# Queries, keys and the output projection by Strassen's scheme, in a two-layer encoder on one core

## The chip, the core and the metric

The kernel runs on one core of a Trainium2 chip. Five engines work side by side, each through its own list of instructions: TensorE (PE, matmuls; its weight loads are shown as PEld), VectorE (DVE), ScalarE (ACT), GpSimd (POOL) and SyncE (SP), which here only issues DMAs. They meet through semaphores. The metric is the device time of one execution in microseconds (us).

## What is computed

An encoder of two layers runs on 512 prompt tokens and 256 sample tokens, with 1024 channels. The weights are the same for both, so the kernel holds all 768 tokens together; only the mixers keep them apart. From the reference:

```python
h = rmsnorm(x, norm_mix_g)
proj = jnp.einsum('bsd,dc->bsc', h, w_in)          # 1024 -> 9760 columns
qa, ka, va, qb, kb, vb, rb, glf, glb, ga, gb = jnp.split(proj, IN_SPLIT_POINTS, axis=-1)
ya = mixer_a(qa, ka, va) @ w_branch_a              # attention, 3 groups x 8 heads x 64
yb = mixer_b(qb, kb, vb, rb, glf, glb, ...) @ w_branch_b   # gated linear attention, 4 heads
merged = sigmoid(ga) * ya + sigmoid(gb) * yb
x = x + merged @ w_out
h = rmsnorm(x, norm_ffn_g)
x = x + square(relu(h @ w_ff1)) @ w_ff2            # 1024 -> 4096 -> 1024
```

Mixer A (attention) has three groups of eight heads: a band of 64 neighbours on either side, and bands on the tokens of every 4th and every 16th position. Each group has its own softmax with a distance penalty, and the groups' outputs are weighted by their softmax denominators. Its queries and keys are 1536 columns each. Mixer B (GLA) has four heads of 128 key and 256 value channels, with a decay per channel, run forward and backward in chunks; its queries and keys are 512 columns each. At the end stands a last rmsnorm.

## The kernel before

Each dense product is taken in fp32r, with both operands split into a hi and a lo half, in three passes (hi x hi, hi x lo, lo x hi) for every 128 rows of the contraction. `Norm` keeps the layer's input times the norm's gain as eight pairs of tiles `hh`, `hl` (128 channels x 768 tokens); the factor per token, `nm.r` (along the free axis) or `nm.rt` (per partition), is multiplied in where a product leaves PSUM.

Two forms take a product from that. `feat_dense` (L243) makes tiles of 128 output columns x tokens: the weight is the stationary operand and 512, then 256 tokens (`SPLITS`) or twice 384 (`HALVES`) stream past it, 24 matmuls each. `tok_dense` (L362) makes tiles of 128 tokens x 256 columns, with the tokens stationary. A weight piece comes by one DMA (`raw`, 2 buffers), is cast on ACT (`whi`, L162) and its rest taken on DVE (`wlo`, L108). The second FFN matrix already goes through `quad_dense` (L326) with operands from `Quads` (L274) and `wquad` (L303): the Strassen-Winograd scheme, which takes seven products of half the size in place of eight, at the cost of sums of quarters of both operands.

The order of the work is set by streams. `add` appends a dense product with the makers of its weights to a stream, `make_units` calls the makers some entries ahead, and `dense_piece` issues the next few matmuls. `weave(steps, total)` (L210) walks through the steps of a mixer and after each issues pieces until the share of `total` us is reached, so PE has matmuls between the steps:

```python
while done < total * (i + 1) / len(steps):
    t = dense_piece()
```

A layer goes like this. Six slices of the attention's values (`tok_dense`, to `v_dram`); the GLA decays (to `la_dram`); queries and keys of head pair 0 (`attention_dense`, L484: six column tiles, evacuated with a multiply by r at L497 to L520). Then four times: the steps of head pair p (`attention_steps`, L525) woven with 44 us of queries and keys of pair p + 1 (`weave(steps, 44)`), behind the last with the dense work of GLA head 0. The steps of a pair are: scores (L590 to L596) with a minimum and a biased copy on DVE (L606) and an exponential with a sum on ACT (L609) for each half; `exchange` stores the sums of groups 1 and 2 to `s_dram`; `combine` (L657) loads them in natural order (`sn`), forms the common weights and sends them back through `l_dram`; probabilities (L615), transposes of them on PE (L621), their split (L624), products with the values (L633). Then four GLA heads (`gla_steps`, L741), each woven with the queries, keys, values and gates of the next head (`gla_dense`, L701), the last one with gate A's eight tiles. Then gate B, `w_branch_a`, `w_branch_b`, the output projection (`feat_dense` with `HALVES`, evacuated at L1168), and the FFN in chunks: up (`feat_dense`), down (`quad_dense`).

After the program is recorded in this order, a scheduler sets the order on each engine. Tiles come from pools: `b3` (36 buffers of 128 x 768), small ones for the mixers (`s1`, `k2`, `lr`, and `dist`, the distance table), and `f3`, `ws` for the FFN, which are opened when the mixers' are closed.

Of the kernel before, what the change touches and what calls it, by code (L numbers as in the profile page):

```python
# [16 lines left out]
DM = 1024  # L17
# [19 lines left out]
V_SLICES = tuple((i * 256, 256 + 32 * (i == 5)) for i in range(6))  # L37
# [39 lines left out]
def encoder(ctx: ExitStack, tc: tile.TileContext, a, y_prompt, y_sample):  # L77
# [19 lines left out]

    def k2(name, dt, tag="k2"):
        return scope[tag].tile([128, 2, 256], dt, tag=tag, name=name)
# [28 lines left out]
    def mixer_constants(pool):  # L128
# [10 lines left out]
        scope.update(dist=dist, cumT=cumT, mask=mask,  # L139
                     glT=pool.tile([98, T], F32R, name="glT"),  # L140
                     wgate=pool.tile([98, 1024], F32R, name="wgate"))
# [3 lines left out]
    l_dram = drm.tile([4, T, 2], F32, name="l_dram")  # L145
    x_dram = drm.tile([DM, T], F32, name="x_dram")
# [28 lines left out]
    def add(makers, body):  # L175
        entry = {"makers": list(makers), "units": [], "body": body}
        stream.append(entry)
        pending.extend((entry, m) for m in entry["makers"])

    def make_units(entry, ahead):  # L180
        while pending and (len(entry["units"]) < len(entry["makers"]) or ahead > 0):
            if len(entry["units"]) == len(entry["makers"]):
                ahead -= 1
# [7 lines left out]
    def dense_piece():  # L191
        while True:
            if not current:
# [3 lines left out]
                make_units(entry, 1)  # L197
# [28 lines left out]

    def feat_tile(unit, ci, x, t0, n, i, evac):
# [3 lines left out]
        ts = slice(t0, t0 + n)  # L231
        yield from mm_group(acc, n, len(x), lambda k: [(w[:, k, c], y[:, ts]) for w, y in passes(hi, lo, *x[k])],
                            3 * n / 2400)
# [9 lines left out]
    def feat_dense(w, c0, x, evac, ncol=128, splits=SPLITS):  # L243

        nkt = len(x)
# [28 lines left out]
    class Quads:  # L274
# [3 lines left out]
        def __init__(self, n):  # L278
            self.n = n
            self.x, self.ops = [None] * n, {}  # L280
            self.b11 = None

        def first(self, p, x):
            if self.b11 is None:
                self.b11 = b3("b11h", F32R, (128, 2, HT)), b3("b11l", F32R, (128, 2, HT))
            self.x[p] = x
            self.ops["B11", p] = split2(x[:, 0:HT], *(y[:, p] for y in self.b11))

        def second(self, p, y):
# [3 lines left out]
            t1, t3, t2, t4 = t13[:, 0:HT], t13[:, HT:T], t24[:, 0:HT], t24[:, HT:T]  # L293
            nc.vector.tensor_tensor(t1, b12, b11, op=ALU.subtract)
            nc.vector.tensor_tensor(t3, b22, b12, op=ALU.subtract)
            nc.vector.tensor_tensor(t2, b22, t1, op=ALU.subtract)
            nc.vector.tensor_tensor(t4, b21, t2, op=ALU.subtract)
            for z, names in ((y, ("B21", "B22")), (t13, ("T1", "T3")), (t24, ("T2", "T4"))):
                hi, lo = split2(z, b3("qh", F32R), b3("ql", F32R))
                for i, name in enumerate(names):  # L300
# [951 lines left out]
```

## Time and profile before

| | us |
|---|---|
| median of 3 runs (lowest, highest) | 3004.87 (3003.84, 3006.55) |
| the profiled execution, whole | 3005.5 |
| its span, first to last instruction | 3003.4 |
| PE busy | 2950.8 (98%) |
| PE weight loads busy | 2791.2 (93%) |
| DVE busy | 1943.3 (65%) |
| ACT busy | 1314.0 (44%) |
| POOL busy | 38.3 (1%) |

The profile was taken in one execution. "Busy" is the time in which an engine's instructions run; PE's records overlap, since matmuls are pipelined, so the step from one matmul to the next is read from long runs of them and not from the mean length of a record. A line such as L223 is the line of the kernel that recorded the instruction; helpers such as L108 (a subtraction that leaves the lo half) serve many places, so the tile names tell where one belongs. The names left of the arrow are written, those on its right are read.

### The profile page before, as it was taken

The page shows a single profiled execution, that of the slowest core. Times are in us where ns is not written, and L with a number is a line of the kernel's source. Part 1 is how long each engine was busy: PE and PEld are TensorE (multiplying, and loading weights), DVE is VectorE, ACT ScalarE, POOL GpSimd, SP SyncE. Part 2 cuts the span into 40 slices and gives each one's busy share as a digit, 9 for nine tenths or more (in the row PEclk, how much of TensorE's full clock was granted, in tenths as well). Part 3 has the DMA queues.
Part 4 walks back from the last instruction along what each step waited for, and adds up shares of the span by engine and source line. Part 5 has one row for each costly group of instructions (what it writes and reads, how often), then busy time and mean ns, then how long its engine had stood idle before and what let it go on. Part 6 is the DMA issues. An engine that isn't in the chain of part 4 may idle for free.

```text
span 3003.4 us, 48678 instructions
## 1 busy us (share of the span) xinstructions
PE 2950.8 (98%) x18908; PEld 2791.2 (93%) x18908; DVE 1943.3 (65%) x4177; ACT 1314.0 (44%) x2790; POOL 38.3 (1%) x119
## 2 busy tenths in 40 slices
PE   8999999999999999999999999999999999999998
PEld 7988889999889999999899888999988899999997
DVE  5456667765445777676953666677754557777767
ACT  4556665444223433333453655655542233333334
POOL 1000000000000000000000000000000000000000
PEclk9999999999999999999999999999999999999998
DMA  6533322222332222222254333322233322222222
GB/s 209 195 83 85 92 79 89 64 72 66 132 101 84 63 71 64 64 66 69 90 191 135 81 86 92 90 92 71 58 110 101 105 64 63 64 64 71 71 61 66
DMA packets 391318, 268.27 MB, mean 89 GB/s; under 512 B 40464, under 2 KB 364464, under 8 KB 391088
## 3 DMA queue, kind: packets, MB, share of 16 engines
q1 hardware_dynamic: 391088, 265.16, 29.8%
q8 instruction: 149, 2.44, 0.3%
q14 instruction: 81, 0.66, 0.1%
HBM read 217.77 MB, written 47.33 MB: 88 GB/s over the span
## 4 chain that ended last, share of the span: by engine, by line
PE 91%; DVE 3%; DMA 3%; ACT 2%; issue 1%; SPq 0%; POOL 0%; DVEq 0%; ACTq 0%
PE acc L223 68%; PE wA L341 8%; PE wC L341 4%; PE wB L341 2%; PE op L633 2%; PE go L850 1%; PE pt L621 1%; PE up L828 1%; PE cp L772 1%; PE ap L810 1%; DMA sn<-s_dram 1%; ACT whi L162 1%; PE sp L596 1%; DVE xT L1206 1%; DMA l_dram<-b 1%
## 5 line engine op out<-in xcount | busy, mean ns | idle before, releaser
L223 PE MATMUL acc<-hh,whi 128*128 128x384 f32 (+2 forms) x2560 | 873.7, 341 | 0.0
L223 PE MATMUL acc<-hl,whi 128*128 128x384 f32 (+2 forms) x2560 | 860.0, 336 | 0.0
L223 PE MATMUL acc<-hh,wlo 128*128 128x384 f32 (+2 forms) x2560 | 859.5, 336 | 0.0
L223 PEld LDWEIGHTS acc<-hh,wlo 128*128 128x128 f32 x2560 | 482.8, 189 | 32.0
L223 PEld LDWEIGHTS acc<-hh,whi 128*128 128x128 f32 x2560 | 483.6, 189 | 26.6
L223 PEld LDWEIGHTS acc<-hl,whi 128*128 128x128 f32 x2560 | 483.9, 189 | 23.0
L162 ACT CAST whi<-raw 128x1024 fp32r<-128x1024 f32 x256 | 268.9, 1050 | 372.8 <-PE acc L223 222.5
L223 PE MATMUL acc<-whi,hh 128*128 128x256 f32 (+1 forms) x1344 | 389.1, 290 | 2.4 <-DVE vst L1004 1.4
L223 PE MATMUL acc<-whi,hl 128*128 128x256 f32 (+1 forms) x1344 | 383.1, 285 | 3.0 <-DVE hl L395 2.8
L223 PE MATMUL acc<-wlo,hh 128*128 128x256 f32 (+1 forms) x1344 | 383.1, 286 | 0.8 <-POOL wlo L108 0.8
L108 DVE TENSOR_TENSOR wlo<-raw,whi 128x1024 fp32r<-128x1024 f32 (+1 forms) x253 | 309.8, 1225 | 84.6 <-ACT whi L162 81.8
L223 PEld LDWEIGHTS acc<-whi,hl 128*128 128x128 f32 x1344 | 258.6, 192 | 5.0 <-DVE hl L395 3.6
L223 PEld LDWEIGHTS acc<-whi,hh 128*128 128x128 f32 x1344 | 258.1, 192 | 4.0 <-issue 2.4
L223 PEld LDWEIGHTS acc<-wlo,hh 128*128 128x128 f32 x1344 | 257.9, 192 | 1.5 <-POOL wlo L108 1.1
L1191 DVE SCALAR_TENSOR_TENSOR rl<-acc,nr 128x384 f32<-128x384 f32 x128 | 70.9, 554 | 187.4 <-PE acc L223 186.1
L1192 ACT ACTIVATE hq<-rl 128x384 f32<-128x384 f32 x128 | 67.1, 524 | 198.3 <-DVE rl L1191 198.2
L1206 DVE TENSOR_TENSOR xT<-xT,wA 128x384 f32<-128x384 f32 x256 | 136.0, 548 | 20.8 <-PE wA L341 19.3
L270 ACT CAST sh<-s 128x512 fp32r<-128x512 f32 x128 | 78.1, 619 | 142.3 <-DVE s L315 80.2
L108 DVE TENSOR_TENSOR ptx<-pt,ptx 128x256 fp32r<-128x256 f32 x192 | 81.0, 422 | 81.8 <-ACT ptx L624 79.3
L223 PE MATMUL acc<-spl,whi 128*128 128x256 f32 (+1 forms) x384 | 129.4, 337 | 0.0
L223 PE MATMUL acc<-sph,whi 128*128 128x256 f32 (+1 forms) x384 | 129.3, 337 | 0.0
L223 PE MATMUL acc<-sph,wlo 128*128 128x256 f32 (+1 forms) x384 | 129.0, 336 | 0.0
(272 smaller groups left out, 5480.6 us busy)
## 6 DMA issues: line engine op xcount, KB each, us to landing
raw<-in_w_in SPq DMA_DIRECT2D x152, 512.0 KB, 3.8
raw<-in_w_ff SPq DMA_DIRECT2D x64, 512.0 KB, 4.1
v_dram<-vst SPq DMA_DIRECT2D x72, 256.0 KB, 3.4
raw<-in_w_ff SPq DMA_DIRECT2D x64, 256.0 KB, 2.9
raw<-in_w_ff SPq DMA_DIRECT2D x128, 128.0 KB, 2.9
v<-v_dram SPq DMA_DIRECT2D x64, 128.0 KB, 4.6
raw<-in_w_branch_b SPq DMA_DIRECT2D x16, 512.0 KB, 4.0
raw<-in_w_out SPq DMA_DIRECT2D x16, 512.0 KB, 4.2
```

Of the source, the lines that this page charges most:

```text
L108: eng.tensor_tensor(out, x, hi.bitcast(F32), op=ALU.subtract)
L162: nc.scalar.copy(hi, raw)
L223: nc.tensor.matmul(acc[:, :n], wt, xt, start=(k == 0 and j == 0), stop=(k == nkt - 1 and j == 2))
L270: nc.scalar.copy(hi, x)
L341: nc.tensor.matmul(acc[:, :HT], x, y, start=(new and p == 0 and j == 0), stop=(p == quads.n - 1 and j == 2), skip_group_check=True)
L596: nc.tensor.matmul(sp[hh][:, (g - 1) * 128:g * 128], q[g][pb, bs], k[g][pb, bs], start=True, stop=True)
L621: nc.tensor.transpose(pt[:, g, hh, :], pr[hh][:, g * 128:(g + 1) * 128], ident)
L633: nc.tensor.matmul(op[:, hh], v[:, hh].rearrange("p s c -> p (s c)"), pT[g][:, hh].rearrange("p s c -> p (s c)"), start=(g == 0), stop=(g ...
L772: nc.tensor.matmul(cp[:, j, :], x[:, j, dc], scope["cumT"][:, d, :], start=(i == 0), stop=(i == 1))
L1191: nc.vector.scalar_tensor_tensor(r, acc[:, :n], 0.0, fnorm.r[:, t0:t0 + n], op0=ALU.max, op1=ALU.mult)
L1192: nc.scalar.activation(q[0][:, t0:t0 + n], r, AF.Square)
L1206: nc.vector.tensor_tensor(x, x, acc, op=ALU.add)
```

## The change

Queries and keys of both mixers (32 column tiles in a layer) become a stage of their own between the first value slices and the attention. `Quads(4)` forms the Strassen operands of the normalised input (x times gain times r, so no product needs r later), and `long_dense` takes two column tiles at a time, a unit: seven products of 4 x 3 matmuls of 384 columns, in the three banks A, B and C, with the weight's sums on DVE and a split for each product. `projections` adds the parts up and stores each finished tile to `p_dram`.

```diff
+    def long_dense(w, units_of, quads, use):
...
+        def load(m):
+            if m % 2:
+                z = [scope["ws"].tile([128, 4, 128], F32, tag="ws", name="wr") for _ in range(4)]
+            else:
+                y = [wraw.tile([128, 8, 128], F32, tag="raw", name="raw8") for _ in range(2)]
...
+        def maker(m, an):
...
+                if m < last and an == "A12":
+                    load(m + 1)
...
+                if an == "S1":
+                    r["S3"] = scope["ws"].tile([128, 4, 128], F32, tag="ws", name="s3")
+                    nc.vector.tensor_tensor(r["S3"], r["A11"], r["A21"], op=ALU.subtract)
+                    nc.vector.tensor_tensor(r["A21"], r["A21"], r["A22"], op=ALU.add)
...
+                op = wsp.tile([128, 8, 128], F32R, tag="w", name="aop")
+                return split2(r[an], op[:, 0:4], op[:, 4:8])
...
+        def product(m, name, bn, bank):
...
+                for p in range(n):
+                    bh, bl = quads.ops[bn, p]
+                    for j, (x, y) in enumerate(passes(ah[:, p], al[:, p], bh, bl)):
+                        nc.tensor.matmul(acc[:, :HT], x, y, start=(new and p == 0 and j == 0),
+                                         stop=(p == n - 1 and j == 2), skip_group_check=True)
...
+                use(m, name, acc[:, :HT])
...
+        for m in range(last + 1):
+            own = [(m, p) for p in ((p1, p2, p5, p6, p3) if m == 0 else (p1, p5, p2, p6, p3))]
+            if m:
+                own.insert(1, (m - 1, p7))
+                own.insert(4, (m - 1, p4))
...
+    def projections(units):
...
+        def total(m, i, half, acc, t):
...
+                elif scale is None:
+                    nc.vector.tensor_tensor(dst, at(acc), at(t), op=ALU.add)
+                else:
+                    nc.vector.scalar_tensor_tensor(dst, at(acc), scale, at(t), op0=ALU.mult, op1=ALU.add)
+            if i != half:
+                nc.sync.dma_start(out=p_dram[row * 128:(row + 1) * 128, :], in_=held.pop((m, i)))
...
+        def normalised(k, x):
+            nc.vector.scalar_tensor_tensor(x, x, gmix[:, l, k:k + 1], nm.r, op0=ALU.mult, op1=ALU.mult)
...
+        long_dense(w_in, [(u[0][0], u[1][0]) for u in units], ops, projections([[c[1:] for c in u] for u in units]))
+        weave(steps, 40 if l else 30)
+        while len(stream) > 7 * len(units):
             dense_piece()
```

The mixers read the finished tiles back. `attention_load` replaces `attention_dense`; its loads and the hi/lo split of group 0 are five steps that are put among the later steps of the pair before, and the load of `sn` is moved ahead of the last three score steps of the band. What fills PE beside the mixers is other dense work: three of the six value slices and gate A's first four tiles (stored to `p_dram`, since the buffers are needed) come beside the head pairs, GLA values and gates beside the GLA heads. These read the same operands through `h_at`, which no longer need a multiply by r. The mixers' pools open only after the new stage, as the stage uses `f3` and `ws`.

```diff
-        return (by_two([u[0] for u in units[1]]) + [exchange] + [u[0] for u in units[0]] + [combine] + [lambda: None] * 4 +
-                skewed([u[1] for kind in (0, 1) for u in units[kind]], 1) + [finish])
+        later_steps = skewed([u[1] for kind in (0, 1) for u in units[kind]], 1)
+        for i, step in enumerate(following):
+            later_steps.insert(8 + 9 * i, step)
+        return (by_two([u[0] for u in units[1]]) + [exchange] + [u[0] for u in units[0][:3]] + [natural] +
+                [u[0] for u in units[0][3:]] + [combine] +
+                [lambda: None] * 4 + later_steps + [finish])
...
+            if p == 0:
+                values(1, False, h_at, False)
+                values(3, False, h_at, False)
+            elif p == 1:
+                values(5, False, h_at, False)
+                gate_a(0, True)
+            elif p == 2:
+                for j in range(1, 4):
+                    gate_a(j, True)
             else:
-                gd = gla_dense(0, w_in, nm, gn)
-            weave(steps, 44)
+                gd = gla_dense(0, w_in, h_at, gn)
+            weave(steps, 24 if p in (1, 2) else 32)
```

The output projection takes the same scheme: `branch_b` in the order 0, 4, 1, 5, 2, 6, 3, 7 forms `merged = Quads(4)`, and `long_dense` has four units, whose products are added to x as they come. The gates' tiles are taken in halves of 384.

```diff
-        feat_dense(a["w_out"][l], 0, mg, evac, ncol=DM, splits=HALVES)
+        long_dense(a["w_out"][l], [(m * 128, (m + 4) * 128) for m in range(4)], merged, use)
```

Two places show what that does to PE's own list of instructions. The first is the scores of the second head pair (first layer): `sp` are scores, `acc` a dense tile. Before:

```order
L596 MATMUL sp<-qk 128x128 x8
L223 MATMUL acc<-hh,whi 128x512
L223 MATMUL acc<-hl,whi 128x512
L223 MATMUL acc<-hh,wlo 128x512
L223 MATMUL acc<-hh,whi 128x512
L223 MATMUL acc<-hl,whi 128x512
L223 MATMUL acc<-hh,wlo 128x512
L596 MATMUL sp<-qk 128x128 x8
```

Now (L737 and L731, L733 are the scores of the dilated groups and of the band; the dense work is a value slice):

```order
L232 MATMUL acc<-whi,ql 128x256
L232 MATMUL acc<-wlo,qh 128x256
L232 MATMUL acc<-whi,qh 128x256
L232 MATMUL acc<-whi,ql 128x256
L737 MATMUL sp<-qk 128x128 x16
L731 MATMUL sp<-qk 128x192
L733 MATMUL sp<-qk 128x192
L731 MATMUL sp<-qk 128x192
L733 MATMUL sp<-qk 128x192
L232 MATMUL acc<-wlo,qh 128x256
L731 MATMUL sp<-qk 128x256 x2
L733 MATMUL sp<-qk 128x256 x2
```

Eight scores stood between runs of six dense matmuls of 512 columns; now 20 follow one another, with single dense matmuls of 256 columns between the next ones.

The second place is the second GLA head of the first layer: `up` are the state updates of the scan, `go` its outputs. Before:

```order
L223 MATMUL acc<-whi,hh 128x256
L223 MATMUL acc<-whi,hl 128x256
L223 MATMUL acc<-wlo,hh 128x256
L828 MATMUL up<-vh,kdh 128x256
L828 MATMUL up<-vl,kdh 128x256
L828 MATMUL up<-vh,kdl 128x256
L223 MATMUL acc<-whi,hh 128x256
```

Now:

```order
L965 MATMUL up<-vh,kdl 128x256
L965 MATMUL up<-vh,kdh 128x256
L965 MATMUL up<-vl,kdh 128x256
L965 MATMUL up<-vh,kdl 128x256
L232 MATMUL acc<-whi,b11l 128x256
L232 MATMUL acc<-wlo,b11h 128x256
L232 MATMUL acc<-whi,b11h 128x256
L232 MATMUL acc<-whi,b11l 128x256
L987 MATMUL go<-vh,ah 128x256
L987 MATMUL go<-vl,ah 128x256
L987 MATMUL go<-vh,al 128x256
L987 MATMUL go<-sh,qh 128x256
```

Updates came in threes, one state's, with dense work on both sides; now several states' stand in a row, and four dense matmuls lie between them and the outputs.

## Rows read from the trace of the kernel before

**Rows 1.** The busy time of each engine (its share of the span, its instructions), and the clock that TensorE was granted in 40 equal slices of the span (tenths, 9 is 0.9 or more).

```profile
PE 2950.8 (98%) x18908; PEld 2791.2 (93%) x18908; DVE 1943.3 (65%) x4177; ACT 1314.0 (44%) x2790; POOL 38.3 (1%) x119
...
PEclk9999999999999999999999999999999999999998
```

**Rows 2.** The chain of waits in order of time: start in us, length in us, engine, tile and line of a piece, and how many instructions it has.

```profile
89.61 13.30 PE acc L223 x111
...
734.35 258.54 PE acc L223 x1494
...
1069.52 24.96 PE acc L223 x144
```

**Rows 3.** TensorE's instructions by line, operands and shape, over the whole run: count, busy time, mean ns of one, idle time just before them. In a shape, 128x512 is a matmul that streams 512 columns. `hh`, `hl` are the hi and lo halves of the normalised input, `mgh`, `mgl` those of the merged branches, `whi`, `wlo` those of a weight. One row of three is shown for each shape; the other two passes have the same counts.

```profile
L223 PE MATMUL acc<-hh,whi 128*128 128x512 f32 x768 | 309.5, 403 | 0.0
...
L223 PE MATMUL acc<-hh,whi 128*128 128x256 f32 x768 | 220.9, 288 | 0.0
...
L223 PE MATMUL acc<-mgh,whi 128*128 128x384 f32 x256 | 85.5, 334 | 0.0
```

**Rows 4.** Busy time of each engine in stretches of the run (start:end, length, then each engine's busy us with its instructions, granted clock, share and rate of the DMA engines). The stretches are the second head pair of the first layer, its second GLA head, a chunk of its FFN, 20 us at the end of its FFN, and 20 us in the second layer's attention.

```profile
257.20:329.60 72.40, 69.65 (x457) 60.67 (x456) 49.47 (x141) 43.86 (x129) 3.85 (x14) 1.00 0.34 88
534.90:601.90 67.00, 67.00 (x521) 64.97 (x520) 47.10 (x121) 33.59 (x85) 0.00 (x0) 1.00 0.24 72
...
1069.50:1132.50 63.00, 63.00 (x362) 62.25 (x361) 46.51 (x84) 21.76 (x33) 0.00 (x0) 1.00 0.23 68
...
1480.00:1500.00 20.00, 17.74 (x87) 16.19 (x88) 19.42 (x41) 11.56 (x22) 0.00 (x0) 0.91 0.31 112
1740.00:1760.00 20.00, 17.68 (x116) 15.08 (x116) 9.86 (x48) 13.82 (x52) 2.38 (x8) 1.00 0.56 137
```

**Rows 5.** What TensorE waited for, over the whole run: its tile and line, the engine and line that ended the wait, us in total, number of waits, the longest.

```profile
PE sp L596 <- DVE s L606: 7.4, 8, 1.0
PE pt L621 <- ACT t L615: 6.2, 6, 2.3
...
PE wA L341 <- DVE xT L1206: 5.4, 5, 1.6
...
PE op L633 <- DVE ptx L108: 1.6, 4, 0.8
```

**Rows 6.** The timeline of the second head pair of the first layer: start, length, engine, line, operation (a wait before it in brackets). First TensorE with the pair's first scores (L596) and first transposes of probabilities (L621), then ScalarE with two neighbouring exponentials of the statistics (L609) from the start of the row of 24.

```profile
257.17 1.16 PE L596 MATMUL sp<-qk 64*128 64x128 f32 x16
...
279.29 0.76 PE L621 MATMUL pt<-eye,t 128*128 128x128 f32 x4 [0.70 <-ACT t L615]
...
260.57 0.51 ACT L609 ACTIVATE junk<-t,s 128x256 f32<-128x256 f32 x1
...
262.01 0.49 ACT L609 ACTIVATE junk<-t,s 128x256 f32<-128x256 f32 x1
```

**Rows 7.** The chain of waits inside 255 to 300 us, from the statistics of the second head pair to its probabilities.

```profile
269.84 1.85 DMA s_dram<-s
...
271.82 3.75 DMA sn<-s_dram
...
276.28 1.04 ACT whi L162
277.35 1.23 DVE wlo L108
```

**Rows 8.** VectorE's instructions in the second head pair (257.2 to 329.6 us) by line and shape: the weight splits, and the first and the last of the eight rows in which queries and keys leave PSUM (L518, L520, L497, L500).

```profile
L108 DVE TENSOR_TENSOR wlo<-raw,whi 128x1024 fp32r<-128x1024 f32 x6 | 7.3, 1224 | 1.2 <-ACT whi L162 1.2
...
L518 DVE SCALAR_TENSOR_TENSOR qk<-acc,qsc,nr 128x512 f32<-128x512 f32 x2 | 2.3, 1140 | 0.0
...
L500 DVE TENSOR_TENSOR qkx<-acc,nr 128x256 f32<-128x256 f32 x1 | 0.4, 425 | 0.0
```

**Rows 9.** The same view of the second GLA head (534.9 to 601.9 us): weight splits, the two lines that end in a multiply by r and a gate (L722, L732), and the first and the last of the four rows in which queries and keys leave PSUM.

```profile
L108 DVE TENSOR_TENSOR wlo<-raw,whi 128x1024 fp32r<-128x1024 f32 x6 | 7.3, 1224 | 2.7 <-ACT whi L162 2.7
...
L732 DVE SCALAR_TENSOR_TENSOR gt<-th,rt,gn 128x256 f32<-128x256 f32 x6 | 2.9, 484 | 0.2
L722 DVE SCALAR_TENSOR_TENSOR vl<-acc,rt,vh 128x256 fp32r<-128x256 f32 x6 | 2.9, 481 | 1.2 <-ACT vh L721 1.2
...
L713 DVE TENSOR_TENSOR gqk<-acc,nr 128x512 f32<-128x512 f32 x1 | 0.7, 684 | 0.0
...
L713 DVE TENSOR_TENSOR gqk<-acc,nr 128x256 f32<-128x256 f32 x1 | 0.4, 415 | 0.0
```

**Rows 10.** Durations over the whole run of the kinds of operation that the new stage is made of, on VectorE (a split of a 128x512 weight sum, of 128x768 and of 128x384, a sum of 128x384) and on ScalarE (a cast of 128x512, a 128x384 pass out of an accumulated tile).

```profile
L108 DVE TENSOR_TENSOR sl<-s,sh 128x512 fp32r<-128x512 f32 x128 | 87.8, 686 | 9.2 <-ACT sh L270 5.5 <-PE wA L341 2.9
...
L108 DVE TENSOR_TENSOR ql<-hq,qh 128x768 fp32r<-128x768 f32 x32 | 30.4, 950 | 0.0
...
L108 DVE TENSOR_TENSOR b11l<-hq,b11h 128x384 fp32r<-128x384 f32 x32 | 17.8, 555 | 5.0 <-ACT b11h L270 4.9
...
L294 DVE TENSOR_TENSOR t<-hq 128x384 f32<-128x384 f32 x32 | 17.5, 548 | 0.0
...
L270 ACT CAST sh<-s 128x512 fp32r<-128x512 f32 x128 | 78.1, 619 | 142.3 <-DVE s L315 80.2 <-PE wA L341 30.7 <-DVE s L318 16.0
...
L1192 ACT ACTIVATE hq<-rl 128x384 f32<-128x384 f32 x128 | 67.1, 524 | 198.3 <-DVE rl L1191 198.2
```

More of the change, by code (lines that the diff above doesn't have):

```diff
@@ L230, in feat_tile @@
         c = slice(ci * 128, (ci + 1) * 128)
-        ts = slice(t0, t0 + n)
-        yield from mm_group(acc, n, len(x), lambda k: [(w[:, k, c], y[:, ts]) for w, y in passes(hi, lo, *x[k])],
-                            3 * n / 2400)
+        yield from mm_group(acc, n, NK if callable(x) else len(x),
+                            lambda k: [(w[:, k, c], y) for w, y in passes(hi, lo, *cols(x, k, t0, n))], 3 * n / 2400)
         evac(i, t0, n, acc)
@@ L525, in attention_steps, with load, others, begin @@
-    def attention_steps(p, q, k):
-        c = p * 128
+        raw = {}
+        def load(tile_, which, g):
+            row = which * 12 + g * 4 + p
+            nc.sync.dma_start(out=tile_, in_=p_dram[row * 128:(row + 1) * 128, :])
+        def others(which):
+            for g in (1, 2):
+                (q, k)[which][g] = b3("qk")
+                load((q, k)[which][g], which, g)
+        def begin(which):
+            raw[which] = b3("qkx")
+            load(raw[which], which, 0)
+        def stacked(which):
+            lst = (q, k)[which]
+            lst[0] = [b3("qk", F32R) for _ in range(2 + 2 * which)]
+            x = raw[which]
+            for hh in range(2):
+                pb, other = slice(hh * 64, hh * 64 + 64), slice(64 - hh * 64, 128 - hh * 64)
+                hi = lst[0][hh]
+                nc.scalar.copy(hi[pb], x[pb])
+                if which:
+                    nc.gpsimd.memset(lst[0][2 + hh][other].bitcast(F32), 0.0)
+                    nc.scalar.copy(hi[other], x[pb])
+                sub((lst[0][2 + hh][pb] if which else hi[other]), x[pb], hi[pb])
@@ L960, in load_x @@
             for j in range(n // 128):
-                t = rows[j, half] = start.tile([128, 512], F32, tag="xin", name="xin")
+                t = rows[j, half] = b3("xin", shape=(128, 512))
                 nc.sync.dma_start(out=t, in_=src[j * 128:(j + 1) * 128, half * 512:(half + 1) * 512])
@@ L1015, in evac @@
                 nc.vector.tensor_copy(gx[:, 96:98], ones[:, 0:2])
[L1016 to L1018 removed]
+            tok_dense(parts, nco, x, evac, order)
+        for i, low_rank in ((0, False), (4, True), (2, False)) if l == 0 else ((4, True), (2, False), (0, False)):
+            values(i, low_rank, nm.h, True, (4, 5, 0, 1, 2, 3) if l == 0 else tuple(range(NT)))
         prefetch()
```

476 lines of the change are left out of this document (293 added, 183 removed).

## The prediction, made before the result was known

> **What bounds the kernel now.** I read the share of busy time first: TensorE (PE) 2950.8 of 3003.4 us, 98%, at nearly the full granted clock, while VectorE (DVE) has 65% and ScalarE (ACT) 44% [rows 1]. So the time is the number of matmul columns that PE streams, plus some 50 us in which PE waits. The chain of waits in order of time gives the price of a column from long runs in which nothing else ends: 111 matmuls of 256 columns in 13.30 us (119.8 ns each), 1494 of alternating 512 and 256 in 258.54 us (173.05 ns), 144 of 384 in 24.96 us (173.33 ns) [rows 2]. The three agree: 0.45 to 0.47 ns a column, so a matmul of 384 costs what a mean one of the 512/256 pair costs, and only the count of matmuls matters. The table of forms gives the counts [rows 3]. The busy time by stage shows where PE has no slack and where the others are near it [rows 4]; the list of PE's waits shows what it waited for [rows 5]. Most of the 15.2 us in attention come from the scores' statistics, the transposes and the value products (7.4 + 6.2 + 1.6).
>
> **What goes: matmuls.** The forms with 512 and 256 columns count 768 each for each of three passes [rows 3], 4608 matmuls. They belong to 48 column tiles in each layer (32 of queries and keys, 16 of the gates), 48 to a tile, so queries and keys of both layers have 2/3 of them: 3072. Times 173.05 ns: 531.6 us. The new stage takes them two column tiles at a time: 16 units per layer, each 7 products of 12 matmuls of 384 columns, 2 x 16 x 84 = 2688, times 173.33 ns = 465.9 us. Gain 65.7. The output projection has 3 x 256 matmuls of 384 [rows 3] and becomes 2 layers x 4 units x 84 = 672: 96 fewer, 16.6 us. The gates change from 512 + 256 to 384 + 384 columns: nothing. Together -82.3. The profiled execution took 3005.5 us (span 3003.4 and 2.1 around it), 0.6 above the median of 3004.87; the sum is made against 3005.5: 2923.2 if every wait stays as it is.
>
> **What it costs: cover.** Queries and keys were also the dense work that filled PE while a head pair's softmax went through DVE, ACT and memory. They are now done ahead, and each stretch has less to fill it.
>
> Attention. A pair now takes 72.4 us with 69.65 of PE [rows 4]; its 288 dense matmuls x 173.05 ns are 49.8, so PE's own work for a pair is 19.8 and 2.8 are waits. The new code gives the four pairs two value slices (288 x 119.8 ns = 34.5), a value slice and a gate tile (17.3 + 8.3), three gate tiles (25.0), and the first GLA head's values and gates (34.5). The chain that counts runs from a pair's first scores to its first transposes of probabilities: 257.17 to 279.29, 22.1 us [rows 6], of which the statistics of 24 halves on ACT at 0.49 us are the larger part, then a store and reload of the sums (1.85 and 3.75 us) and the combine, in which a weight's split stood (1.04 + 1.23 us) [rows 7]. The program before put 45 matmuls of 512 and 24 of 256 on PE in that stretch: 45 x 226.3 ns (2 x 173.05 - 119.8) + 24 x 119.8 = 13.1 us, and the scores themselves about 7.3 (22.1 less the 13.1 and 1.7 of waits). By the order of the new program that stretch holds 12 matmuls of 384 and 90 of 256 in the first pair (12.9 us), 53 of 256 in the second (6.4), 32 of 384 in the third (5.5), 77 of 256 in the fourth (9.2), and in the last three also three value products of the pair before (0.4). The chain itself gets shorter, as the reload is queued before the last scores and fewer weight splits stand in it: between 18 (3.4 us start, 24 x 0.49, and some 3 for bubbles and the combine) and 22.1 as now; I take 20. PE's program reaches the transposes after 20.2, 14.1, 13.2 and 16.9 us, so it waits 0, 5.9, 6.8 and 3.1, and with the 1.1 of smaller waits that a pair has now, 20.2 per layer, 40.4 in all against 15.2: **+25** (at 18: +10; at 22.1: +42). In the second pair DVE has 49.5 - 9.4 (the eight evacuation rows of queries and keys) - 3 x 1.224 (splits) + 3 (value splits, gate copies) = 39.4 of 45.4 us, 87% [rows 8]: full, not over.
>
> GLA heads. A head takes 67.0 us with no wait [rows 4]; without its 96 query and key matmuls (16.6) 50.4. DVE's 47.1 lose two weight splits (2.4), the evacuations of queries and keys (2.2) and the multiply by r (about 0.7): 41.8 [rows 9], 83%. The nearest rows are an FFN chunk with DVE at 74% where PE lost nothing and the 20 us from 1480 with DVE at 97% where PE lost 2.26 us, 11% [rows 4]. Between them by the share, 83% loses 4.4%, 2.2 us a head; the order shows the updates of several states in a row with no dense work between them, which speaks for a loss. I take 2: **+16** for 8 heads (bounds 0 and 5.7 a head, the 11%).
>
> Clock. In the 20 us from 1480 the granted clock was 0.91, in those from 1740, with as little PE work, 1.00 [rows 4]: not the share decides but how the idle time lies. One such drop costs 1.8 us (0.09 x 20). The four longest new waits (second and third pair, both layers) may each bring one; I take half: **+4** (0 to 7). The Trainium skill ("TensorE: Matmul & The Clock Gate", section "HAM oscillation — how this bites in real kernels") says that a kernel which makes PE wait in every round pays for the cold clock in every round. By that rule all 16 pairs and heads would pay: 29 us in place of 4, a rival below; the 1.00 from 1740 speaks against it for short waits, and the longer ones have no row here.
>
> Handover. Before the new stage the normalised input is formed and split: per pair of rows 2 x 950 ns, one split of 555, four sums of 550 and three splits of 950 ns, 7.5 us, 30 us of DVE in all [rows 10], woven into 30 us (layer 1) or 40 us (layer 2) of value work that itself has some 9 to 12 us on DVE. Layer 1 is up to 9 us late, of which the first two products cover 4; layer 2 about in time. **+6** (0 to 16). After the last product, the distance table is fetched into memory that the stage held: **+4** for two layers (0 to 10, a transfer of 3.75 us [rows 7] and its issue). The merged operands before the output projection: the last pair's 7.5 us of DVE lie behind the last branch tile, partly under the first products, **+4** (0 to 10).
>
> The new stage itself: a unit is 84 x 173.33 = 14.56 us of PE against seven splits (686 ns), four sums of the same size and some 2.3 of totals on DVE, 9.9 us, 68%; ACT seven casts (619) and four copies (524), 6.4 [rows 10]. That is below the FFN chunk's 74%, where nothing was lost: 0 (upper bound 11%, 1.6 a unit). Its weights, 1 MB per unit in 14.6 us, are 72 GB/s, and the 32 stores of 384 KB a layer lie under it. The loads of queries and keys for a pair are issued during the pair before, 20 us and more ahead of use, and cost nothing.
>
> Sum: 2923.2 + 25 + 16 + 4 + 6 + 4 + 4 = **2982 us**, 0.8% faster: of 82 us of matmuls taken away some 59 come back as waits.
>
> **The rivals.**
> A, everything stays hidden: the recorded order puts other work into the waits, only the matmuls go. For it: GLA and FFN rows without any wait [rows 4]. Against it: the 22.1 us chain with 14 us on top of it. 2923 with all waits as before, up to 2950 with the attention term alone.
> B, slower: the mixers' chains become the bound. If the attention chain keeps its 22.1 (+42) and each GLA head loses 11% of its time (5.7, +46), with the other terms as taken the time is 2923 + 42 + 46 + 4 + 14 = 3029. With attention as forecast it is slower than before from 4.9 us a head: (82.3 - 25 - 4 - 14) / 8. For it: DVE at 83 to 87% with ACT in turn with it; against it: no wait at all now in the heads.
> C, the stage of queries and keys is bound by DVE, ACT or weights: 1 us a unit is 32 us, 3014. For it: the products of the FFN waited 5.4 us for one kind of sum [rows 5]; against it: that is under 0.1 us for each of their 64 groups.
> D, the cold clock after every wait: 2982 + 25 = 3007.
> That the change does not do what it says can be left out: the order holds the 2688 and 672 matmuls.
>
> **How the numbers follow.** Forecast 0.52 (its own range 2950 to 2999; 0.50 faster, 0.02 the same), A 0.21 (faster), B 0.14 (0.02 same, 0.12 slower), C 0.08 (0.02, 0.03, 0.03), D 0.05 (0.01, 0.02, 0.02). About 0.2% is what a measurement of this kernel can tell from no change: 2999 to 3011. So faster 0.74, same 0.09, slower 0.17. The range, 2922 to 3025, reaches to A's lower end and to B's near end.
>
> **What would show it.** Right: PE busy near 2870, PE idle near 110 us in all; from first scores to first transposes 18 to 20 us in the second and third pair with a PE wait of 5 to 7 just before; heads of 51 to 54 us; units of the new stage at 14.6 us. Wrong: heads over 56 us or a clock under 0.95 over a whole head (B, D); units over 15.5 us (C); transposes without a wait (A).

## The result and the profile after

The changed kernel takes 3025.47 us (median of 4 runs, 3024.01 to 3028.84) against 3005.71 for the kernel before in the same series: a ratio of 1.0068, 95% interval 1.005 to 1.0085. It is slower, where 0.8% faster was forecast. The page of the profiled execution (span, busy times, granted clock in 40 slices) answers to [rows 1]:

```profile
span 3024.6 us, 49070 instructions
...
PE 2912.0 (96%) x18428; PEld 2832.2 (94%) x18428; DVE 2151.7 (71%) x4607; ACT 1447.1 (48%) x3104; POOL 38.4 (1%) x119
...
PEclk9999999999999999999999999999999999999998
```

PE is busy 39 us less on the page, where 82.3 us of matmuls went, and the span is 21 us longer. PE's idle time grew from 52.6 to 112.6 us (span less busy), and the mean granted clock of the span fell from 0.995 to 0.986. To see where the time lies I cut both runs at the same places of the program: the first matmul of the second layer, and in each layer the first attention score, the first GLA matmul, the first matmul of branch A, the first product of the second FFN matrix. The columns are those of [rows 4]. Before, first and second layer:

```profile
0.00:186.80 186.80, 174.40 (x1224) 163.73 (x1224) 86.10 (x173) 81.07 (x150) 10.45 (x15) 0.98 0.56 179
186.80:474.40 287.60, 280.73 (x1933) 250.49 (x1933) 197.92 (x572) 180.77 (x522) 12.45 (x48) 1.00 0.33 85
474.40:788.50 314.10, 314.10 (x2254) 296.49 (x2253) 204.59 (x500) 147.89 (x354) 0.00 (x0) 1.00 0.27 84
788.50:1031.50 243.00, 243.00 (x1398) 227.03 (x1397) 127.08 (x195) 77.73 (x117) 0.00 (x0) 1.00 0.26 80
1503.80:1664.70 160.90, 160.90 (x1180) 153.97 (x1180) 76.00 (x147) 66.70 (x117) 2.94 (x8) 1.00 0.50 162
1664.70:1953.30 288.60, 280.11 (x1933) 250.46 (x1933) 198.14 (x572) 180.96 (x522) 12.45 (x48) 1.00 0.33 85
1953.30:2267.40 314.10, 314.10 (x2253) 296.44 (x2253) 204.09 (x499) 147.96 (x354) 0.00 (x0) 1.00 0.27 84
2267.40:2510.40 243.00, 243.00 (x1398) 227.05 (x1397) 127.11 (x195) 77.73 (x117) 0.00 (x0) 1.00 0.27 80
```

After:

```profile
0.00:332.10 332.10, 309.38 (x1834) 302.62 (x1834) 235.33 (x414) 169.94 (x314) 9.04 (x9) 0.98 0.49 157
332.10:564.80 232.70, 211.31 (x1612) 201.25 (x1612) 157.66 (x525) 165.53 (x506) 13.93 (x54) 0.96 0.52 155
564.80:811.10 246.30, 236.23 (x1771) 232.89 (x1770) 171.39 (x466) 130.80 (x342) 0.00 (x0) 0.97 0.33 107
811.10:1047.20 236.10, 235.97 (x1350) 221.72 (x1349) 154.69 (x250) 88.70 (x136) 0.00 (x0) 1.00 0.26 78
1521.00:1823.60 302.60, 294.74 (x1794) 291.23 (x1794) 223.87 (x388) 154.20 (x281) 1.47 (x2) 0.99 0.46 148
1823.60:2050.50 226.90, 210.38 (x1612) 200.78 (x1612) 157.91 (x525) 165.37 (x506) 13.93 (x54) 0.97 0.53 159
2050.50:2296.80 246.30, 235.67 (x1772) 232.35 (x1771) 171.33 (x465) 131.05 (x342) 0.00 (x0) 0.98 0.33 107
2296.80:2532.80 236.00, 236.00 (x1350) 221.81 (x1349) 154.88 (x250) 88.81 (x136) 0.00 (x0) 1.00 0.26 78
```

Read the length of each stretch against the matmuls that moved, at the prices of [rows 2], for one layer. "Lost" is by how much the stretch is longer than that, for both layers together.

| stretch | matmuls moved | measured, layer 1 and 2 | lost |
|---|---|---|---|
| values, queries and keys | +233.0 (new stage) - 49.8 (pair 0) - 51.8 (three slices) = +131.4 | +145.3, +141.7 | 24.2 |
| attention | - 149.5 - 16.6 + 51.8 + 33.3 = -81.0 | -54.9, -61.7 | 45.4 |
| GLA heads to gate B | - 49.8 - 33.3 = -83.1 | -67.8, -67.8 | 30.6 |
| branches, output projection, first FFN tiles | -8.3 | -6.9, -7.0 | 2.7 |
| rest | 0 | +1.5, -1.2 | 0.3 |

The stretches lose 103 us together; 82.3 of matmuls went. That is the 21 us. The list of PE's waits (whole run) says where the idle part of it lies; it answers to [rows 5]:

```profile
PE acc L232 <- ACT sgb L618: 20.4, 2, 10.5
PE pt L762 <- ACT t L756: 19.5, 6, 4.6
PE pt L762 <- issue: 8.1, 2, 4.5
PE op L774 <- DVE ptx L117: 6.3, 12, 1.8
PE acc L232 <- DVE gx L1155: 6.2, 4, 3.9
...
PE wA L431 <- ACT u L475: 3.9, 2, 2.0
```

The first line is new. The second and third were 6.2 us in all, the fourth 1.6.

Five stretches of the changed kernel settle some of the forecast's conditions: the stage of queries and keys, the GLA heads, and three places just behind a wait.

```profile
110.00:332.00 222.00, 221.10 (x1265) 220.10 (x1264) 154.06 (x242) 115.97 (x208) 1.47 (x2) 1.00 0.46 150
566.00:757.50 191.50, 191.34 (x1523) 188.41 (x1522) 152.01 (x434) 110.36 (x307) 0.00 (x0) 1.00 0.29 88
360.00:363.40 3.40, 3.40 (x18) 3.40 (x17) 1.27 (x3) 3.05 (x10) 0.00 (x0) 0.50 0.02 0
470.50:476.00 5.50, 4.97 (x19) 4.83 (x20) 1.74 (x4) 4.36 (x13) 0.00 (x0) 0.50 0.08 2
787.40:793.60 6.20, 6.16 (x19) 6.16 (x20) 0.59 (x1) 0.75 (x2) 0.00 (x0) 0.51 0.01 3
```

The new stage is as forecast: 221.1 of 222.0 us PE is busy. The heads have no wait. Behind these three waits PE works at a granted clock of 0.50, the lower of its two levels, so such a wait costs more than its own length.

### The profile page after: what moved, and what is told of

The parts are those of the page before. It is cut to its first block, busy times and chain, and to the rows that moved or that the text cites. A ratio compares the mean times of both kernels' runs of the same rounds, so it can differ in the third digit from the quotient of the medians.

```text
span 3024.6 us, 49070 instructions
## 1 busy us (share of the span) xinstructions
PE 2912.0 (96%) x18428; PEld 2832.2 (94%) x18428; DVE 2151.7 (71%) x4607; ACT 1447.1 (48%) x3104; POOL 38.4 (1%) x119
## 4 chain that ended last, share of the span: by engine, by line
PE 84%; DVE 6%; DMA 3%; ACT 3%; issue 2%; SPq 1%; POOL 0%; DVEq 0%; ACTq 0%
PE acc L232 44%; PE wA L431 11%; PE wA L357 8%; PE wC L431 5%; PE wC L357 4%; PE wB L431 3%; PE wB L357 2%; PE go L987 1%; PE op L774 1%; PE pt L762 1%; PE sp L737 1%; DMA sn<-s_dram 1%; PE cp L909 1%; DMA raw<-in_w_in 1%; PE ap L947 1%
## 5 line engine op out<-in xcount | busy, mean ns | idle before, releaser
L232 PE MATMUL acc<-hh,whi 128*128 128x384 f32 x1024 | 345.7, 338 | 0.0
L232 PE MATMUL acc<-hh,wlo 128*128 128x384 f32 x1024 | 344.2, 336 | 0.0
L232 PE MATMUL acc<-hl,whi 128*128 128x384 f32 x1024 | 343.7, 336 | 0.0
L170 ACT CAST whi<-raw 128x1024 fp32r<-128x1024 f32 (+1 forms) x176 | 185.4, 1053 | 293.3 <-PE acc L232 184.9
L431 PE MATMUL wA<-qh,aop 128*128 128x384 f32 x960 | 262.6, 340 | 4.9 <-ACT u L475 3.9
L232 PEld LDWEIGHTS acc<-hl,whi 128*128 128x128 f32 x1024 | 192.1, 188 | 0.9 <-DVE hl L546 0.4
L232 PEld LDWEIGHTS acc<-hh,whi 128*128 128x128 f32 x1024 | 192.2, 188 | 0.3
L232 PEld LDWEIGHTS acc<-hh,wlo 128*128 128x128 f32 x1024 | 192.2, 188 | 0.3
L431 PEld LDWEIGHTS wA<-qh,aop 128*128 128x128 f32 x960 | 177.1, 190 | 7.0 <-ACT u L475 4.4
L431 PE MATMUL wC<-qh,aop 128*128 128x384 f32 x640 | 178.3, 337 | 1.2 <-ACT aop L281 1.1
```

The lines of the kernel that those rows point to most:

```text
L170: nc.scalar.copy(hi, raw)
L232: nc.tensor.matmul(acc[:, :n], wt, xt, start=(k == 0 and j == 0), stop=(k == nkt - 1 and j == 2))
L431: nc.tensor.matmul(acc[:, :HT], x, y, start=(new and p == 0 and j == 0), stop=(p == n - 1 and j == 2), skip_group_check=True)
```

## The experiments

All times stand beside runs of the kernel before on the same chip. Since the chips differ a little, kernels are compared by their ratios to it; 0.001 is 3.0 us, and a ratio's interval is 0.001 to 0.002 on either side. The changed kernel has 1.0068.

**What makes gate B wait.** The chain of waits at the end of the first layer's GLA heads, in the changed kernel (start, length, what):

```profile
769.27 0.51 SPq L1343
...
769.83 0.43 SPq L623
...
770.31 6.57 DMA spl<-ma_dram
...
777.00 0.97 DVE spl L626
...
777.99 0.84 ACT sph L628
...
785.18 0.96 DVE spl L626
...
786.90 0.49 ACT sgb L618
```

SP issues three of the four reloads of gate A (L1343) only behind the last stores of the GLA, then the loads of branch A's input (L623). The first of those land at 776.9. VectorE and ScalarE then add and split four tiles, and only behind the fourth does ScalarE come to the first gate tile of gate B (`sgb`), whose bank PE waits for. PE stood from 777.5 to 787.4.

e1_gates:

```diff
-            gate(ta[j], ta[j])
-        xa = [split_from((ma_dram[0], ma_dram[1]), j, f3, f3) for j in range(4)]
+        gate_steps = [f for j in range(4) for f in (lambda j=j: split_a(j), lambda j=j: gate(ta[j], ta[j]))]
...
+        for _ in range(6):
+            dense_piece()
+        weave(gate_steps, 28)
```

> The four reloads of gate A are issued where they were, but their tanh on ScalarE and the four splits of branch A's input are spread among gate B's first four tiles instead of standing ahead of them. Theory W (between the GLA heads and gate B, TensorE has no dense work left and gate B's evacuations stand in ScalarE's list behind four reloaded tanh and four splits; 10 us of wait and some 7 us at half clock per layer): 28 to 34 us less than the changed kernel, 2991 to 2998 us, and no wait of acc on sgb over 1 us. Rival R (the transfers of branch A's input land too late by themselves): the wait moves to branch A, 0 to 8 us less.

Measured: 3011.29 us, ratio 1.0014 (1.0004 to 1.0023), 16 us below the changed kernel. The wait on `sgb` fell from 20.4 us to 3.6. That is about half of what theory W expected, and no wait on branch A's input came in its place.

e2_reload moves the tanh alone:

> Only the tanh of the four reloaded gate A tiles is moved behind gate B's first tiles; the splits of branch A's input stay ahead of gate B as in the changed kernel. If the reload is what makes gate B wait: 20 us or more below the changed kernel (3005 or less). If it is the splits, which the kernel before had there too, and only the dense work that covered them is gone: 0 to 8 us less (3017 to 3026).

Measured: 3030.92, ratio 1.0079 (1.0064 to 1.0094), 3 us above; the wait on `sgb` is still 19.9 us. The tanh of the reloaded tiles is not the cause. The splits are, which e1_gates moved too, and they stood there in the kernel before as well.

e3_cover:

```diff
-            weave(steps, 32)
+            weave(steps, 32 if hd < 3 else 16)
```

> The last GLA head's steps are woven with 16 us of gate A instead of 32, so some 17 us of dense work stand behind them, as 22 us did in the kernel before (66 us of gate A, 44 woven). Nothing else moves. Theory W in its form 'the cover is gone': 20 to 33 us less (2992 to 3005). Rival: order on ScalarE alone decides, or the head now starves by as much: 0 to 8 us less.

Measured: 3026.72, ratio 1.0074 (1.0056 to 1.0091): nothing gained. PE's waits of this kernel show why:

```profile
PE tp L1016 <- DVE o L1008: 6.7, 2, 3.4
...
PE acc L232 <- ACT sgb L618: 4.7, 2, 2.8
```

The work left behind the last head covered the splits (20.4 to 4.7 us), but the last head, which had lost it, now waits 6.7 us for its output norm. The cover is short at both ends. The two do not balance: the GLA stretches became 3.4 and 0.7 us shorter, which the whole time does not show above its noise.

e9_gates24 is e1_gates with 24 pieces of gate B (11.5 us) ahead of the first split in place of 6, since that split still stood in front of gate B's first evacuations.

> e1_gates with the first split 24 pieces of gate B (11.5 us) behind its start in place of 6. If the 44 us of e11_sum are the sum of its parts, this part has to bring more than e1_gates did: 20 to 26 us below the changed kernel (ratio to the kernel before 0.998 to 1.000), with no wait of acc on sgb. If e1_gates already had all there was in it: 13 to 17 us below (ratio 1.001 to 1.0025), and e11_sum's parts help one another.

Measured: 3007.79, ratio 1.0004 (0.9994 to 1.0014), 19 us below the changed kernel. It lies between the two, 3 us better than e1_gates, which the intervals do not separate. No wait on `sgb` is left among PE's longest, and the stretches from the first GLA matmul to branch A take 234.0 and 233.5 us in place of 246.3 each: there 25 of the 30.6 us lost are back.

**The handover to the new stage.** e4_spread:

```diff
-        weave(steps, 40 if l else 30)
+        weave(steps, 46 if l else 38)
```

> Forming and splitting the normalised input before the stage of queries and keys is spread over 38 and 46 us of the value slices in place of 30 and 40. Theory H (the handover costs some 15 us a layer because those 30 us of VectorE work crowd out the evacuations of the values): 6 to 15 us less (3010 to 3019). Rival (VectorE is full there whatever the spread, 84 to 94% of the stretch): within 3 us of the changed kernel, or slower as the first product starts later.

Measured: 3012.91, ratio 1.0013 (1.0003 to 1.0022), 17 us below the changed kernel, more than expected. The waits on the low-rank tile (`gx`, `gl`), 6.8 us in layer 1, fell to 1.3. Values of the first layer from 20 us on (columns as above):

```profile
20.00:72.00 52.00, 46.88 (x356) 44.32 (x355) 46.19 (x105) 29.57 (x60) 2.00 (x1) 1.00 0.67 221
```

VectorE is 89% busy there and PE 90%. In the same 52 us of the changed kernel VectorE was busy 47.43 us, 91%, and PE only 42.27, 81%. So VectorE's load in this stretch hardly changed; with the steps of the forming further apart, the evacuations for which PE waited came sooner.

**The first head pair.** From first scores to first transposes (the wait of [rows 6]) the second pair took what was forecast:

```profile
397.23 0.71 PE L737 MATMUL sp<-qk 64*128 64x128 f32 x8
...
415.97 0.41 PE L762 MATMUL pt<-eye,t 128*128 128x128 f32 x2 [2.38 <-ACT t L756]
```

18.7 us, where it was 22.1 before; in the third pair 19.6, in the fourth 22.5 (second layer 18.7, 19.9, 21.8). The first pairs took 27.1 and 25.2. Their chain:

```profile
334.70 4.20 DMA dist<-in_alibi
...
338.92 0.42 DVE t L747
...
349.66 5.04 PE acc L232 x42
354.70 4.54 issue
```

The distance table lands at 338.9, 6.8 us after the first scores at 332.1; PE then has its program until 354.7 and waits 4.5 us.

e5_dist loads the table into a buffer of `b3` during the stage of queries and keys:

> The distance table is loaded into another buffer during the stage of queries and keys, not after its last product; the rest is the changed kernel. Theory T (the first pair of each layer waits 4.5 and 3.5 us before its first transposes because the table lands 6.8 us after its first scores, and the clock falls with it, 5 us): 8 to 13 us below the changed kernel (3012 to 3017), and first scores to first transposes near 21 us in the first pair. Rival (the load of the sums stands in SP's list behind fourteen loads of values, so the chain stays as long): 0 to 3 us less.

Measured: 3022.42, ratio 1.0049 (1.0034 to 1.0064), 6 us below, which the intervals do not separate, and the chain still took 25.8 and 26.0 us. Neither theory named what the chain shows now:

```profile
332.51 4.78 DMA mats<-in_mats
...
337.31 0.43 DVE cumT L144
...
351.87 6.22 issue
```

The copies of the GLA's constants (`cumT`, L144) stand ahead of the first biased scores in VectorE's list, and wait for their load.

e10_dist2 moves these too:

```diff
-            q1, k1, following = attention_load(p + 1) if p < 3 else (None, None, [])
+            q1, k1, following = attention_load(p + 1) if p < 3 else (None, None, [gla_constants])
```

> The distance table is loaded during the stage of queries and keys, as in e5_dist, and the GLA's constants (two loads and two VectorE copies that stood ahead of the first pair's scores) are loaded and copied beside the fourth pair. Theory V (in e5_dist the first biased scores still waited, because the copies stand ahead of them in VectorE's list and their load landed 5 us after the first scores): from first scores to first transposes 20 to 22 us in both first pairs instead of 25 to 27, and 8 to 13 us below the changed kernel. Rival S (the load of the sums behind fourteen loads of values in SP's list): 24 us or more, and no more than e5_dist's 5 us below.

Measured: 3023.68, ratio 1.0059 (1.0039 to 1.0079), 3 us below the changed kernel; the chain is 23.1 and 23.9 us. Between theory V and rival S, and the gain is inside the noise: PE still waits 4.5 and 5.3 us there. Rival S's cause is not seen in the first layer's chain: the load of the sums is issued at 347.7, 0.1 us behind the end of their store, and takes 4.40 us. What holds the last 3 us was not followed further.

**The output projection.** e6_plain_out takes this part alone back.

> The output projection alone is as in the kernel before (768 matmuls of 384, merged branches split once per tile), the rest is the changed kernel. If the Strassen form keeps what it saves (16.6 us of matmuls): 12 to 17 us above the changed kernel (3037 to 3042). If its handover eats it, as the forecast allowed 4 of it: 5 to 12 above. If it gains nothing: within 3.

Measured: 3043.48, ratio 1.0118 (1.0101 to 1.0135), 15 us above the changed kernel. This half of the change keeps nearly all of its 16.6 us.

**What a head pair costs.** e8_dummy puts idle matmuls where PE waits:

```diff
+                for _ in range(7):
+                    nc.tensor.matmul(z, y[:, 0, 0:128], y[:, 1, 0:256], start=True, stop=True)
...
-                [lambda: None] * 4 + later_steps + [finish])
+                [fill] * 4 + later_steps + [finish])
```

> The changed kernel with 28 extra matmuls of 256 columns (3.35 us) between a pair's last scores and its first transposes, into a bank that nothing reads: 26.8 us more work for TensorE in all, put where it waits 27.6 us in all. Theory C (each such wait also costs because the clock falls behind it: 31 us at half clock in the attention of both layers, 15 us lost): 8 to 14 us below the changed kernel (3011 to 3017) in spite of the added work, and no half clock in the second to fourth pair. Rival (the half clock has another cause or costs nothing): 0 to 5 us above it. If the waits could not be filled at all: 20 us or more above.

Measured: 3046.28, ratio 1.0127 (1.0111 to 1.0142), 18 us above the changed kernel, so some 9 of the 26.8 us found room: between the rival's 0 to 5 and the 20 of waits that cannot be filled. PE's waits:

```profile
PE op L774 <- DVE ptx L117: 18.1, 17, 2.5
...
PE pt L762 <- ACT t L756: 5.3, 3, 2.5
```

The wait on the transposes fell from 19.5 us to 5.3, and the wait on the split probabilities (`ptx`) rose from 6.3 to 18.1. The clock still fell to its lower level in the second to fourth pairs. Theory C falls: behind the first wait stands a second, and filling the first does not spare the clock.

e7_shift gives the second and third pair one more gate tile each, on top of e1_gates:

> On top of the kernel with the reloads spread among gate B: two more of gate A's tiles (8.3 us each) are computed beside the second and third head pair, stored and reloaded, and the last GLA head keeps two, woven with 16 us. Theory K (the attention pairs lack cover, the GLA heads have enough): 8 to 20 us below that kernel (2991 to 3003). Rival (the cover is short everywhere, so what the pairs gain the last GLA head and gate B lose): within 4 us of it, or slower.

Measured: 3024.29, ratio 1.0054 (1.0039 to 1.0069), 12 us above e1_gates. The attention of the first layer took 233.6 us in place of e1_gates' 235.9 although it had 16.6 us more to do (in the second layer 232.7 in place of 230.0), but at gate B PE waited 28.7 us in two waits. The rival's case.

**Together.** e11_sum has e9_gates24, e4_spread and e10_dist2 in one.

> Three mends together: the reloads and splits spread among gate B (with 24 pieces of gate B ahead of the first), the forming of the input spread over 38 and 46 us, and the constants as in e10_dist2. If the three losses are separate: 3025 less 14, 12 and 10, so 2984 to 2996, faster than the kernel before. If what one gains another loses again: 3000 or more.

Measured: 2982.04 us, ratio 0.9915 (0.9893 to 0.9937): 46 us below the changed kernel, 0.85% faster than the kernel before. It is 2 us below the range that was expected of separate losses; the parts measured one by one give 19 + 17 + 3 = 39. First layer, the same four stretches:

```profile
0.00:321.90 321.90, 306.33 (x1834) 299.68 (x1834) 234.36 (x414) 168.83 (x314) 9.03 (x9) 0.99 0.51 162
321.90:550.00 228.10, 210.82 (x1616) 201.18 (x1616) 157.68 (x529) 165.71 (x506) 13.93 (x54) 0.96 0.54 159
550.00:783.40 233.40, 233.09 (x1769) 230.03 (x1768) 170.75 (x462) 130.63 (x342) 0.00 (x0) 1.00 0.36 113
783.40:1019.30 235.90, 235.90 (x1349) 221.70 (x1348) 154.85 (x250) 88.69 (x136) 0.00 (x0) 1.00 0.27 78
```

Against the changed kernel the first stretch is 10.2 us shorter, attention 4.6, the GLA 12.9. This version beats both. What came back is the handover and gate B: of attention's loss in this layer, 26.1 us by the table's sum, 21.5 are still there.

e12_sum_shift adds e7_shift's two tiles:

> e11_sum, and two more of gate A's tiles beside the second and third pair, as in e7_shift. There the attention's loss fell by 19 us in the first layer and 14 in the second, and came back at gate B (14 us of wait and 20 us at half clock), because the first split stood ahead of gate B's first evacuations. With 24 pieces ahead of it, theory K (a pair takes 50 to 56 us whatever dense work it holds, so more of it is nearly free) expects 15 to 33 us below e11_sum. Rival (the last GLA head needs that work as cover): within 5 us of e11_sum, or slower.

Measured: 3002.84, ratio 0.9991 (0.9981 to 1.0001), 23 us above e11_sum. The second and third pair took 59.4 and 57.3 us in place of 51.4 and 52.9, the last GLA head waited again for its norm (3.3 us in each layer), and gate B for its evacuations (8.7 us in all). The rival's case, and more: here the added work was not hidden in the pairs either.

e13_bare takes all dense work out of the third pair:

> e11_sum, with the three gate A tiles (25.0 us of dense work) taken out of the third head pair and computed beside the last GLA head, without store and reload; the third pair has no dense work of its own left. The pair has 20 us of TensorE work by itself and takes 52 us in e11_sum. Theory L (a pair is a chain through ScalarE, VectorE and memory of some 19 us up to its first transposes and 28 to 32 behind them, whatever PE has to do): the third pair still takes 44 to 52 us, and the kernel is 30 to 44 us slower than e11_sum (3012 to 3026). Rival M (the pairs are long because dense work and its evacuations crowd them): the third pair takes 25 to 35 us, and the kernel is within 15 us of e11_sum.

Measured: 3009.29, ratio 1.0003 (0.9994 to 1.0013), 26 us above e11_sum. The third pair of the first layer, from its first scores to those of the fourth:

```profile
435.70:484.50 48.80, 37.14 (x232) 32.09 (x231) 33.84 (x122) 37.03 (x118) 4.16 (x15) 0.78 0.50 148
```

48.8 us (47.6 in the second layer), where it was 52.9 (51.9) with its 25.0 us of dense work. The scheduler drew 7.3 us of the fourth pair's dense work into it, so it was not quite bare: 27 us of work at full clock, for which PE is busy 37 us at a clock of 0.78. That is theory L's length and not rival M's: some 21 us to the first transposes and 28 behind them, and 17.7 us less dense work made the pair only 4 us shorter. One thing is not separated: with so little to do PE ran much of the pair at its lower clock, its own transposes and products too, so it is not shown that the chain would be as long at the full clock. The kernel as a whole lost less than the 30 it was to lose at least. The stretches from the first GLA matmul to branch A grew by 24.9 and 24.7 us, the whole of the 25.0 moved there, while attention got 12.7 and 15.1 us shorter. In the first layer 7.6 of them are the fourth pair's, from which the 7.3 us of dense work had been drawn: dense work was nearly free in the third pair, not in the fourth.

## Why the prediction was wrong

The forecast was 2982 with 59 us of the 82.3 coming back as waits; 103 came back. First by kind. Of the 59, 55 were idle time and 4 the clock. PE's idle time grew by 60 (near 110 us in all was named as a sign of being right, and it is 112.6), so the sum of the waits came out; most of their places did not, so that is luck. PE's busy time was to be near 2870 and is 2912.0: some 43 us came back inside it, against the clock's 4. By the mean granted clock (0.014 of 3024.6 us missing, before 0.005 of 3003.4) some 27 of them at most are work at the lower level; what the rest is, no run separates. Then by place:

- **Matmuls, -82.3: right.** e6_plain_out gives 15 of the 16.6 us of the output projection; the new stage runs with 0.9 us of waits in 222. The condition for rival C did not arise.
- **Output projection's handover, +4: right.** 2.7.
- **GLA heads, +16: wrong, and the wait that took its place had no term.** The heads lost nothing (191.34 of 191.5 us busy), although VectorE was 79% busy. The 30 us came behind the last head. The forecast moved four of gate A's eight tiles and took that as neutral for time. In the kernel before, 66 us of gate A were woven into 44 us of the last head, and the 22 left over lay over the loads and splits of branch A's input; now 33 us are woven into 32. The step that failed is the count of what else a moved tile covered: 20.4 us of wait at gate B, with the lower clock behind it, and e9_gates24 took 25 of the 30 us in these stretches back by order alone. Rival B forecast 3029, near the result, but by another mechanism, and is wrong with it.
- **Handover to the new stage, +6 (0 to 16): 24.** The mechanism was right, the size not: the sum took only how late the first product's operands are. The rest was paid beside it, by the evacuations behind the sums in VectorE's list, the low-rank tile's most of all; e4_spread took 17 us of it away with two numbers.
- **Attention, +25, with clock +4 and distance table +4: 45.** The chain taken at 20 us (18 to 22.1) measured 18.7 to 22.5 in the second to fourth pairs of both layers, and the second and third pair took 54.2 and 52.4 us in the first layer, against 45.4 + 7.0 and 44.8 + 7.9 by the forecast's terms. The error in length is the first pair: 65.1 and 62.8 us (2.1 of each are the last twelve products of the new stage), where the terms give 54.3 + 1.1, while none of the other six is over by more than 2.5. It was given no wait at all, at 20.2 us of cover over a chain of 20; the chain was 27.1 and 25.2. The forecast had priced the table's transfer, 2 us a layer, and not that ScalarE's 24 statistics start behind it. Without the table and the constants behind the last product the chain is 4.0 and 1.3 us shorter (e10_dist2), but PE's wait is not; what makes the rest stays open. Here too the waits as such came out: idle time grew from 15.4 to 37.9 us, 22.5 for the 25, with 8.1 before the first pairs' transposes, where 0 was forecast, and 19.5 before the others', where 31.6 was. The remaining 23 us are busy time. (By the forecast's own terms the bound at a chain of 18 is +13, not +10.)
- **Clock, +4 (0 to 7): up to 27.** This is the second step that failed, by its size. The price of a drop, 1.8 us from the row at 0.91, was near (the stretches at 0.50 above cost half of 3.4 to 6.2 us each), but only four drops were counted, half of them paid. Eleven came that the kernel before does not have at these places: with six of the eight waits before first transposes, with both at gate B, and three in the handovers (two in layer 1, one in layer 2). The Trainium skill ("TensorE: Matmul & The Clock Gate", section "HAM oscillation — how this bites in real kernels") tells of a loop in which a wait for a transfer in each round throws the clock back, so that every round starts at the lower one. The trace agrees in part: all five waits of 3.3 us and more ahead of first transposes were followed by a drop, of the three of 2.3 to 2.7 us one was. Rival D's 29 us for the clock is nearer than the forecast's 4, though not by its rule, since the heads, half of its rounds, had no wait.
- **The range** ended at 3025, half a microsecond below the result, because its upper end was one mechanism (the mixers' chains) and left out a wait at a place that no term named.

What stays open: why the first pair's chain keeps 23 us in e10_dist2, what the busy time holds beyond the lower clock (16 us or more), and whether the 7 us by which e11_sum beats the sum of its parts are more than noise.

## What to carry to other kernels

Before work is moved, list every place that it covered, also the serial stretch right behind it: the 22 us of dense work past the end of a loop hid 10 us of loads and splits, and no row of the old profile showed a wait there. Where a stage's end, a queue of loads and a list of evacuations meet, the order within one engine's list decides: the same work, spread by two numbers of a weave and two moved blocks, was worth 46 us, and turned 0.7% slower into 0.85% faster. Price the clock with the waits: here a sum of waits that was right came with up to 27 us of slower work where 4 were counted. A chain such as this softmax through memory kept nearly its length when its cover was taken away, and grew when more was added (e12_sum_shift); give it as much dense work as it can hide and no more, and look for the rest of the cover elsewhere.

## What the runs showed that was not expected

A head pair with 20 us of TensorE work of its own takes 48 to 49 us with 7 us of dense work beside it and 52 to 53 with 25. And waits filled with idle matmuls hid about a third of them: 26.8 us added, some 9 hidden.
